# A decoder block on one core: gates evaluated one product late, attention outputs loaded earlier, w_out in two interleaved couples

## The chip, the core and the metric

The kernel runs on one core of a Trainium2 chip. A core has five engines with an instruction queue each, worked off in order: TensorE (PE, matrix products, with its weight loads PEld beside them), VectorE (DVE), ScalarE (ACT), GpSimd (POOL) and SyncE (SP), which here issues every DMA transfer. An engine that comes to an instruction whose inputs are not there waits, and all that is queued behind it on that engine waits too. Products are collected in PSUM, eight banks of 128x512 numbers; all else lies in SBUF. The metric is the time of one execution in microseconds (us), the median of three runs: 1360.38 us before (1358.13 to 1365.16).

## The reference

All is float32; sequence and model width are 1024, the FFN width is 2816. Cut to what matters here:

```
u    = rmsnorm(x, norm1_g)
proj = u @ w_in          # aq, ak, av, mqk, mv, mo, mi, mf, ga, gm
ya   = sliding_window_attention(aq, ak, av, sinks) @ w_attn_branch
h    = mlstm_chunkwise(silu(conv(mqk)), mv, mi, mf)      # 8 chunks of 128
h    = rmsnorm(h) * sigmoid(mo)
ym   = h @ w_mlstm_branch
x    = x + (sigmoid(ga) * ya + sigmoid(gm) * ym) @ w_out
f    = rmsnorm(x, norm2_g)
x    = x + (silu(f @ w_ffn_gate) * (f @ w_ffn_up)) @ w_ffn_down
out  = rmsnorm(x, final_norm_g)
```

## The kernel before

Activations lie transposed (channels on the partitions, 1024 tokens along the row, cut in two halves of 512). Every float32 operand is split into a rounded part and the rest (`split`: ACT writes the first, DVE or POOL the second, line 72/73), and each product is three matmuls: high by high, high by low, low by high (lines 776 to 778 and 108 to 110).

The program goes in stages. First the input projections with attention and the mLSTM recurrence (about 0 to 345 us in the trace); beside the recurrence, whose chunks are the loop over `c`, two of the four operand groups for the next stage are prepared (`u_load`, `operand`). Then the gates mo and gm (345 to 472), the two branch products (472 to 574; "o" is the attention output, "hh/hl" the split of the gated h), w_out with the residual (574 to 740), the FFN's gate and up products (740 to 1300) and the down projection.

Gates, w_out and FFN use a Strassen-Winograd scheme. A *pair* n is a 256-row block of weights against all 1024 tokens; its 2x2 block product needs seven products instead of eight, numbered 1 to 7, each of 12 matmuls of 128x512 (`seven`). A pair gives four quarters ij = 0 to 3, each 128 channels by 512 tokens. Pairs 0 to 5 are the gates (PG), 6 to 9 are w_out (PO), 10 to 31 the FFN (PF). `product7` runs one product and combines its sums: product 1 is copied to "v" (line 801), product 5 to "d" (806), "w" (809, then POOL in 810) is quarter 3, "c" (817) are quarters 1 and 2. Even pairs collect in banks "mm" and odd ones in "mb" (three each), product 5 in "st" (two). `prep` makes a product's weights four products ahead: sums "s_" on POOL (line 760), then a split into "whi"/"wlo" (five buffers each). `load_pair` reads a pair's weights from memory: "wraw" (two buffers) and "wr2" ("wr" in the trace; two blocks).

The order of products is the list SEQ: the first two pairs of a stage are interleaved (`first_two`), the others follow one by one in ORDER. Work is recorded in program order and each engine's queue follows it closely; so where the recording of a pair's loads, of a sigmoid or of a store stands sets where it comes in the queue.

Three consumers matter. In the gates, `out_gate` multiplies a quarter by Rt (line 824, on DVE for quarters 0 and 1, on POOL for the others), takes the sigmoid on ACT (825) and either multiplies h (829) or stores gm to memory (827). Line 849 (`load_o`) reads the attention output back after product 7 of the last gate pair, `split_o` splits it beside products 2 and 3, and the loop behind the gates' stage splits h. In w_out, `out_x` adds the residual "xr" (line 944, on DVE for quarter 0, on POOL for the others), writes the FFN's operand "f" (ACT, 947), and passes the previous quarter to `to_tokens`: four PE transposes into an "st" bank (922), copies by ACT and DVE (927, 929), four squares with sums on ACT (932) and a store. All operands that the FFN derives from f are made beside the products of pair 9 (`last_x`).

Of the kernel before, what the change touches and what calls it, by code (L numbers as in the profile page):

```python
# [17 lines left out]
D = 1024  # L18
# [14 lines left out]
def hybrid_block(ctx, tc, xT, xt, par, g3row, cst, abias, w_fm, w_mv, w_br, w_pr, w_dn, out):  # L33
# [621 lines left out]
    for a, b in ((PO, PF), (PF, PN)):  # L655
        SEQ += first_two(a, (1, 5), (6, 7), (2, 3, 4)) + [(n, i) for n in range(a + 2, b) for i in ORDER]
# [23 lines left out]
    def u_load(kt, late=False):  # L680
        for k in (2 * kt, 2 * kt + 1):
# [6 lines left out]
            else:  # L688
                U_[k] = blk("xz")
                nc.sync.dma_start(out=U_[k], in_=xT[k])  # L690
                A.activation(U_[k], U_[k], AF.Copy, scale=scale)

    ml_a(0)
    run(gai)
    for c in range(NT):
        if c + 1 < NT:
            ml_a(c + 1)
        ml_b(c)
        run(gai)
        if c > 0:  # L700
            ml_c(c - 1)
        if c in (2, 5):
            u_load(c // 3)
        if c in (3, 6):
            for i in (5, 6, 7, 4):
                operand("u", i, c // 3 - 1, U_)
# [31 lines left out]
    def load_pair(n):  # L738
# [4 lines left out]
        r.append([half("wr2", "hs", 3), half("wr2", "hs", 3)] if n == PG + 1 else blk("wr2"))  # L743
        for i in range(2):
            if n == PG + 1 and i:
# [6 lines left out]
    def prep(g):  # L752
        n, i = SEQ[g]
        if i == 6 and n + 1 not in (PG + 1, PO, PO + 1, PF, PF + 1):
            load_pair(n + 1)
# [64 lines left out]

    def out_gate(n, ij, c):
        j, h = 2 * n + ij // 2, ij % 2
        dst = c if ij else ev_("c")
        (V if ij in (0, 1) else G).tensor_tensor(dst, c, Rt[:, hs(h)], ALU.mult)
        A.activation(dst, dst, AF.Sigmoid)
        if j >= 4:
            nc.sync.dma_start(out=gmd[j - 4, :, hs(h)], in_=dst)
            return
# [32 lines left out]
    for g in range(NSG):  # L861
# [3 lines left out]
        if g in (0, 1, 3, 8):  # L865
            todo_u.pop(0)()
        product7(n, i, lambda n, ij: ev_("c"), out_gate)
        if n == PO - 1:
            if i == 7:
# [4 lines left out]
            elif i in (2, 3):  # L874
                split_o(i - 2, 0)
                split_o(i - 2, 1)
                if i == 2:
                    wt_y[0] = weights(w_br[0], 4)

# [39 lines left out]
    def to_tokens(xc, j, h):  # L919
        pt = st_ps()  # L920
        for t in range(4):
            T.transpose(pt[:, t * P:(t + 1) * P], xc[:, t * P:(t + 1) * P], idn)
        x_, junk = work("x2"), work("junk")
# [6 lines left out]
        for t in range(4):  # L930
            c = slice(t * P, (t + 1) * P)
            A.activation(junk[:, c], x_[:, c], AF.Square, accum_out=ss2[:, h * 4 + t, j:j + 1])
# [8 lines left out]
    def out_x(n, ij, c):  # L941
# [7 lines left out]
        if len(later) > 1:  # L949
# [71 lines left out]
    def dprep(c):  # L1021
# [11 lines left out]
        elif i == 4:  # L1033
# [6 lines left out]
    last_x = {1: [(1, 0), (1, 1)], 6: [(1, 2), (5, 0)], 5: [(5, 1), (5, 2)], 7: [(6, 0), (6, 1)],  # L1040
              2: [(1, 3), (6, 2), (7, 0)], 3: [(5, 3), (6, 3)], 4: [(7, 1), (7, 2), (7, 3)]}
    res_at = {1: 3, 6: 0, 5: 1, 7: 2}
    prep(NSG + 2)
    prep(NSG + 3)
    for g in range(NSG, len(SEQ)):
# [3 lines left out]
        if n < PF:  # L1049
            if i in res_at:  # L1050
# [194 lines left out]
```

## Time and profile before

| | before |
|---|---|
| median of 3 runs | 1360.38 us |
| the profiled execution | 1365.96 us, span 1364.2 us |
| PE busy | 1297.9 us, 95% of the span |
| DVE, ACT, POOL busy | 61%, 45%, 45% |
| granted TensorE clock, mean | 0.98 |

The span runs from the first to the last instruction of the profiled execution; what lies around it is 1.8 us. Times in rows are us from the span's start. PE is busy nearly always, so what can be won on the other engines shows only where PE has a gap, or where it works at the lower granted clock. A PE instruction's own duration includes its drain: in a run of 128x512 matmuls each starts about 0.23 us behind the last.

### The profile page before, as it was taken

Reading aid. Unit: us, or ns where it says so; the run is one execution under the profiler, and the core shown is the slowest. Engines: PE = TensorE matmul, PEld = TensorE weight load, DVE = VectorE, ACT = ScalarE, POOL = GpSimd, SP = SyncE. Lnnn points to the kernel's source line nnn. Section 1 sums busy time; section 2 is a strip of 40 time slices with the busy share of each in tenths; the row PEclk is TensorE's granted clock in tenths of the full one; section 3 lists DMA queues with packets and bytes.
Section 4 is the critical chain, followed back from the end, with each engine's and each line's share of the span. In section 5 each row is a group of like instructions: output and inputs, shape, how many; then the busy total and the mean of one; then the engine's idle time right before and its main releaser. Section 6 shows DMA issues by size and latency. Waiting matters only on the chain.

```text
span 1364.2 us, 17154 instructions
## 1 busy us (share of the span) xinstructions
PE 1297.9 (95%) x5970; PEld 1052.6 (77%) x5970; DVE 837.8 (61%) x1335; ACT 619.7 (45%) x1271; POOL 613.5 (45%) x480
## 2 busy tenths in 40 slices
PE   9999999999999979979779999999999999999986
PEld 7888998777777768857668888888888888888865
DVE  5369763566854464575795555556555565664795
ACT  5369864356523442247663333333233343555322
POOL 0245533231644333554556655566556535700470
PEclk9999999999999989989989999999999999999998
DMA  8111113302312453214413222332322249973761
GB/s 323 55 60 33 48 32 121 119 31 93 131 39 88 170 200 131 90 49 135 123 47 103 86 101 101 116 116 101 116 72 91 101 155 324 343 261 93 258 216 62
DMA packets 77799, 168.31 MB, mean 123 GB/s; under 512 B 8080, under 2 KB 16528, under 8 KB 77712
## 3 DMA queue, kind: packets, MB, share of 16 engines
q1 hardware_dynamic: 77712, 167.22, 35.8%
q8 instruction: 47, 0.77, 0.2%
q14 instruction: 40, 0.33, 0.1%
HBM read 128.13 MB, written 39.06 MB: 123 GB/s over the span
## 4 chain that ended last, share of the span: by engine, by line
PE 48%; DVE 6%; POOL 3%; ACT 3%; issue 2%; DMA 2%; SPq 0%; DVEq 0%; POOLq 0%; ACTq 0%
PE mm L777 6%; PE mm L778 6%; PE mm L776 5%; PE mb L777 5%; PE mb L776 5%; PE mb L778 5%; PE st L776 4%; PE st L777 4%; PE st L778 4%; DVE xzl L73 1%; DMA ld<-hd__5307 1%; PE mb L110 1%; PE mb L108 1%; PE mb L109 1%; DVE wlo L73 1%
## 5 line engine op out<-in xcount | busy, mean ns | idle before, releaser
L73 DVE TENSOR_TENSOR xzl<-ld,xzh 128x1024 fp32r<-128x1024 f32 x77 | 116.3, 1540 | 65.2 <-ACT xzh L72 53.3
L72 ACT ACTIVATE whi<-wraw 128x512 fp32r<-128x512 f32 (+1 forms) x124 | 77.2, 627 | 132.0 <-PE st L777 46.6
L73 DVE TENSOR_TENSOR wlo<-wraw,whi 128x512 fp32r<-128x512 f32 (+1 forms) x96 | 80.5, 841 | 42.4 <-ACT whi L72 42.3
L72 ACT ACTIVATE xzh<-ld 128x1024 fp32r<-128x1024 f32 x77 | 79.6, 1055 | 58.0 <-DMA ld<-in_w_dn_dram 18.6
L810 POOL TENSOR_TENSOR w<-w,d 128x512 f32<-128x512 f32 x32 | 50.3, 1572 | 119.4 <-DVE w L809 109.1
L108 PE MATMUL mm<-uh,whi 128*128 128x512 f32 x256 | 103.4, 407 | 0.5 <-ACT whi L72 0.5
L109 PE MATMUL mm<-ul,whi 128*128 128x512 f32 x256 | 102.2, 400 | 0.0
L110 PE MATMUL mm<-uh,wlo 128*128 128x512 f32 x256 | 101.9, 398 | 0.0
L776 PE MATMUL mb<-zf,whi 128*128 128x512 f32 x220 | 87.6, 398 | 0.0
L778 PE MATMUL mb<-zf,wlo 128*128 128x512 f32 x220 | 87.3, 397 | 0.1
L777 PE MATMUL mb<-zf,whi 128*128 128x512 f32 x220 | 87.3, 397 | 0.0
L776 PE MATMUL mm<-zf,whi 128*128 128x512 f32 x220 | 86.9, 395 | 0.0
L777 PE MATMUL mm<-zf,whi 128*128 128x512 f32 x220 | 86.8, 394 | 0.0
L778 PE MATMUL mm<-zf,wlo 128*128 128x512 f32 x220 | 86.7, 394 | 0.0
L776 PE MATMUL st<-zf,whi 128*128 128x512 f32 x176 | 70.2, 399 | 0.0
L777 PE MATMUL st<-zf,whi 128*128 128x512 f32 x176 | 70.1, 398 | 0.0
L778 PE MATMUL st<-zf,wlo 128*128 128x512 f32 x176 | 69.9, 397 | 0.0
L981 ACT ACTIVATE sg<-sg 128x512 f32<-128x512 f32 x44 | 27.7, 629 | 74.6 <-DVE sg L980 38.3
L108 PEld LDWEIGHTS mm<-uh,whi 128*128 128x128 f32 x256 | 49.1, 192 | 12.5 <-ACT whi L72 1.8
L110 PEld LDWEIGHTS mm<-uh,wlo 128*128 128x128 f32 x256 | 48.9, 191 | 11.6 <-DVE wlo L73 0.2
L777 PE MATMUL mm<-xzl,xzh 128*128 128x512 f32 x132 | 53.0, 402 | 4.9 <-DVE xzl L73 4.9
L109 PEld LDWEIGHTS mm<-ul,whi 128*128 128x128 f32 x256 | 49.0, 192 | 10.3
(766 smaller groups left out, 3805.0 us busy)
## 6 DMA issues: line engine op xcount, KB each, us to landing
ld<-hd__5307 SPq DMA_DIRECT2D x77, 256.0 KB, 4.6
lz<-in_w_dn_dram SPq DMA_DIRECT2D x66, 256.0 KB, 5.3
wraw<-in_w_pr_dram SPq DMA_DIRECT2D x32, 512.0 KB, 3.7
wr<-in_w_pr_dram SPq DMA_DIRECT2D x31, 512.0 KB, 5.5
hd__5307<-hs SPq DMA_DIRECT2D x44, 256.0 KB, 2.1
hd__5307<-sg SPq DMA_DIRECT2D x33, 256.0 KB, 2.3
ld<-in_w_dn_dram SPq DMA_DIRECT2D x33, 256.0 KB, 4.5
wraw<-in_w_fm_dram SPq DMA_DIRECT2D x16, 512.0 KB, 3.8
```

What stands on the lines that cost most here:

```text
L72: A.activation(hi, src, AF.Copy)
L73: eng.tensor_tensor(lo, src, hi.bitcast(F32), ALU.subtract)
L108: T.matmul(ps, ah, bh, start=(i == 0), stop=False)
L109: T.matmul(ps, ah, bl, start=False, stop=False)
L110: T.matmul(ps, al, bh, start=False, stop=(i == n - 1))
L776: T.matmul(ps, xh, zh, start=start, stop=False, skip_group_check=more)
L777: T.matmul(ps, xh, zl, start=False, stop=False, skip_group_check=more)
L778: T.matmul(ps, xl, zh, start=False, stop=stop, skip_group_check=more)
L810: G.tensor_tensor(e["w"], e["w"], e["d5"], ALU.subtract)
L981: A.activation(dst, dst, AF.Silu)
```

## The change

SEQ runs pairs 8 and 9 interleaved like 6 and 7. Their weights are loaded behind product 4 of pairs 6 and 7. In the gates the odd pairs 1, 3 and 5 put their second weight block into two half tiles ("hs") instead of a wr2 block, with one DMA each; the sigmoid of a quarter is recorded one product later than its multiply and a gm store one more (`late`). The attention output is loaded after product 1 of pair 5 instead of product 7 and split one block per product. `u_load` scales x on POOL instead of ACT, and its pieces are spread over chunks 2 to 6. In w_out, transposes go into "mm"/"mb" banks, a quarter waits two places instead of one in `later`, and the square is written back into the bank (no "junk" tile); the FFN operands are spread over the products of pairs 8 and 9 (`early_f`), and the residual is loaded by a list (`need`), three quarters ahead.

```diff
--- before.py
+++ after.py
@@ -652,8 +652,9 @@
 
     SEQ = first_two(PG, (1,), (2,), (5,), (6, 7), (3, 4)) + [(n, i) for n in range(PG + 2, PO) for i in ORDER]
     NSG = len(SEQ)
-    for a, b in ((PO, PF), (PF, PN)):
-        SEQ += first_two(a, (1, 5), (6, 7), (2, 3, 4)) + [(n, i) for n in range(a + 2, b) for i in ORDER]
+    for a in (PO, PO + 2, PF):
+        SEQ += first_two(a, (1, 5), (6, 7), (2, 3, 4))
+    SEQ += [(n, i) for n in range(PF + 2, PN) for i in ORDER]
     fz = {}
 
     def z_of(n):
@@ -688,22 +689,22 @@
             else:
                 U_[k] = blk("xz")
                 nc.sync.dma_start(out=U_[k], in_=xT[k])
-                A.activation(U_[k], U_[k], AF.Copy, scale=scale)
+                G.tensor_scalar(U_[k], U_[k], scale, 1.0, ALU.mult, ALU.mult)
 
     ml_a(0)
     run(gai)
+    pieces = [lambda kt=kt, i=i: operand("u", i, kt, U_) if i else u_load(kt) for kt in range(2) for i in (0, 5, 6, 7, 4)]
     for c in range(NT):
         if c + 1 < NT:
             ml_a(c + 1)
+        if 2 <= c < 7:
+            pieces.pop(0)()
         ml_b(c)
         run(gai)
         if c > 0:
             ml_c(c - 1)
-        if c in (2, 5):
-            u_load(c // 3)
-        if c in (3, 6):
-            for i in (5, 6, 7, 4):
-                operand("u", i, c // 3 - 1, U_)
+        if 2 <= c < 7:
+            pieces.pop(0)()
     ml_c(NT - 1)
     run(gai, 16)
     ph_a.close()
@@ -740,9 +741,10 @@
         if n in raws or n >= PN:
             return
         r = [wp.tile([P, 1024], F32, name="wraw", tag="wraw", bufs=2)]
-        r.append([half("wr2", "hs", 3), half("wr2", "hs", 3)] if n == PG + 1 else blk("wr2"))
+        odd = n < PO and n % 2
+        r.append([half("wr2", "hs", 3), half("wr2", "hs", 3)] if odd else blk("wr2"))
         for i in range(2):
-            if n == PG + 1 and i:
+            if odd and i:
                 for k in range(2):
                     nc.sync.dma_start(out=r[i][k], in_=w_pr[n, i, :, hs(k)])
             else:
@@ -751,7 +753,9 @@
 
     def prep(g):
         n, i = SEQ[g]
-        if i == 6 and n + 1 not in (PG + 1, PO, PO + 1, PF, PF + 1):
+        if (n, i) in ((PO, 4), (PO + 1, 4)):
+            load_pair(n + 2)
+        elif i == 6 and n + 1 not in (PG + 1, PF + 1) and not PO <= n + 1 <= PF:
             load_pair(n + 1)
         x11, x12, x21, x22 = raws[n]
 
@@ -818,13 +822,18 @@
             out(n, ij, c)
 
 
+    late = []
+
     def out_gate(n, ij, c):
         j, h = 2 * n + ij // 2, ij % 2
         dst = c if ij else ev_("c")
         (V if ij in (0, 1) else G).tensor_tensor(dst, c, Rt[:, hs(h)], ALU.mult)
+        late.append(lambda: sig_gate(dst, j, h))
+
+    def sig_gate(dst, j, h):
         A.activation(dst, dst, AF.Sigmoid)
         if j >= 4:
-            nc.sync.dma_start(out=gmd[j - 4, :, hs(h)], in_=dst)
+            late.append(lambda: nc.sync.dma_start(out=gmd[j - 4, :, hs(h)], in_=dst))
             return
...
@@ -864,18 +873,24 @@
             prep(g + LA)
         if g in (0, 1, 3, 8):
             todo_u.pop(0)()
+        now = late[:]
         product7(n, i, lambda n, ij: ev_("c"), out_gate)
+        for f_ in now:
+            late.remove(f_)
+            f_()
         if n == PO - 1:
-            if i == 7:
+            if i == 1:
                 for h in range(2):
                     for p in range(2):
                         load_o(h, p)
                 load_g(0)
-            elif i in (2, 3):
-                split_o(i - 2, 0)
-                split_o(i - 2, 1)
+            elif i in (5, 7, 2, 3):
+                k = (5, 7, 2, 3).index(i)
+                split_o(k // 2, k % 2)
                 if i == 2:
                     wt_y[0] = weights(w_br[0], 4)
+    while late:
+        late.pop(0)()
...
@@ -917,10 +932,10 @@
     F_, xres, later = {}, {}, []
 
     def to_tokens(xc, j, h):
-        pt = st_ps()
+        pt = bank(j // 2 % 2, 0)
         for t in range(4):
             T.transpose(pt[:, t * P:(t + 1) * P], xc[:, t * P:(t + 1) * P], idn)
-        x_, junk = work("x2"), work("junk")
+        x_ = work("x2")
         for q in range(2):
             c = slice(q * 256, (q + 1) * 256)
             if q == 0:
@@ -929,7 +944,7 @@
                 V.tensor_copy(x_[:, c], pt[:, c])
         for t in range(4):
             c = slice(t * P, (t + 1) * P)
-            A.activation(junk[:, c], x_[:, c], AF.Square, accum_out=ss2[:, h * 4 + t, j:j + 1])
+            A.activation(pt[:, c], pt[:, c], AF.Square, accum_out=ss2[:, h * 4 + t, j:j + 1])
         nc.sync.dma_start(out=x2d[h * 4:(h + 1) * 4, :, j * P:(j + 1) * P].rearrange("t p c -> p t c"),
                           in_=x_.rearrange("p (t c) -> p t c", t=4))
 
@@ -946,7 +961,7 @@
             F_[j] = blk("f")
         A.activation(F_[j][:, hs(h)], xc, AF.Copy, scale=prm[:, C_G2 + j:C_G2 + j + 1])
         later.append((xc, j, h))
-        if len(later) > 1:
+        if len(later) > 2:
             to_tokens(*later.pop(0))
 
 
@@ -1037,9 +1052,14 @@
         dop[c] = hi, lo
 
     todo = [("m", i, kt, mg) for i in (6, 7, 2, 3, 4) for kt in range(4)]
-    last_x = {1: [(1, 0), (1, 1)], 6: [(1, 2), (5, 0)], 5: [(5, 1), (5, 2)], 7: [(6, 0), (6, 1)],
-              2: [(1, 3), (6, 2), (7, 0)], 3: [(5, 3), (6, 3)], 4: [(7, 1), (7, 2), (7, 3)]}
-    res_at = {1: 3, 6: 0, 5: 1, 7: 2}
+
+    early_f = {(PO + 2, 5): [(1, 0)], (PO + 3, 1): [(1, 1)], (PO + 3, 5): [(5, 0)], (PO + 2, 6): [(5, 1)],
...
+    need = [(n + k, ij) for n in (PO, PO + 2) for k, ijs in ((0, (3,)), (1, (3,)), (0, (0, 1, 2)), (1, (0, 1, 2))) for ij in ijs]
+    for _ in range(3):
+        load_res(*need.pop(0))
...
@@ -1047,18 +1067,16 @@
         if g + LA < len(SEQ):
             prep(g + LA)
         if n < PF:
-            if i in res_at:
-                load_res(n, res_at[i])
-            if n == PF - 1 and i == 6:
-                load_pair(PF)
-            if n == PF - 1 and i == 2:
-                load_pair(PF + 1)
+            if (n, i) in ((PF - 1, 7), (PF - 1, 2)):
+                load_pair(PF + (i == 2))
             product7(n, i, lambda n, ij: ev_("c"), out_x)
-            if n == PF - 1:
-                for i_, kt in last_x[i]:
-                    operand("f", i_, kt, F_)
-                if i == 4:
-                    todo = [("f", i_, kt, F_) for i_ in (2, 3, 4) for kt in range(4)]
+            if i in (7, 2, 3, 4) and need:
+                load_res(*need.pop(0))
+            for i_, kt in early_f.get((n, i), ()):
+                operand("f", i_, kt, F_)
+            if (n, i) == (PF - 1, 4):
+                todo = [("f", 2, kt, F_) for kt in range(4)] + [("f", 3, kt, F_) for kt in (2, 3)]
+                todo += [("f", 4, kt, F_) for kt in range(4)]
         else:
             if i == 1 and n % 2 == 0:
                 sgs[n] = sgs[n + 1] = [x for _ in range(2) for x in halves(blk("sg"))]
@@ -1068,8 +1086,9 @@
             product7(n, i, dst_h, out_h)
             if later:
                 to_tokens(*later.pop(0))
-                V.tensor_reduce(rstd2, ss2, mybir.AxisListType.X, ALU.add)
-                rstd_of(rstd2, rstd2, D, NT)
+                if not later:
+                    V.tensor_reduce(rstd2, ss2, mybir.AxisListType.X, ALU.add)
+                    rstd_of(rstd2, rstd2, D, NT)
         if n == PN - 1 and i in (7, 2, 3):
             for c in {7: range(LP), 2: range(2), 3: range(2, LP)}[i]:
                 (dload if i == 7 else dprep)(c)
```

SP's queue in the gates, before (gmd are the gm stores, wr and wraw weights, o the attention output; wr_4112 and wr_4265 are the second blocks of pairs 4 and 5):

```order
L827 DMA gmd<-c 128x512
L749 DMA wr_4112<-in_w_pr_dram 128x1024
L827 DMA gmd<-w 128x512
L827 DMA gmd<-c 128x512 x2
L81 DMA wraw<-in_w_br_dram 128x512
L827 DMA gmd<-c 128x512
L749 DMA wr_4265<-in_w_pr_dram 128x1024
L827 DMA gmd<-w 128x512
L827 DMA gmd<-c 128x512 x2
L849 DMA o<-od 128x1024
L827 DMA gmd<-c 128x512
L849 DMA o<-od 128x1024 x3
```

and now:

```order
L751 DMA wraw<-in_w_pr_dram 128x1024
L749 DMA wr_4265<-in_w_pr_dram 128x512
L749 DMA wr_4266<-in_w_pr_dram 128x512
L751 DMA wraw<-in_w_pr_dram 128x1024
L751 DMA wr_4112<-in_w_pr_dram 128x1024
L836 DMA gmd<-w 128x512
L836 DMA gmd<-c 128x512 x2
L751 DMA wraw<-in_w_pr_dram 128x1024
L836 DMA gmd<-c 128x512
```

Both blocks now stand ahead of the first gm store, and pair 5's in two halves. ACT at the third of the gate pairs, before (whi is the split of a weight sum, L825 the sigmoid):

```order
L806 ACTIVATE d_4086<-st 128x512
L72 ACTIVATE whi<-s__4117 128x512
L825 ACTIVATE w<-w 128x512
L72 ACTIVATE whi<-s__4115 128x512
L825 ACTIVATE c<-c 128x512
L72 ACTIVATE whi<-s__4160 128x512
L825 ACTIVATE c<-c 128x512
```

and now:

```order
L810 ACTIVATE d_4088<-st 128x512
L72 ACTIVATE whi<-s__4117 128x512
L834 ACTIVATE w<-w 128x512
L72 ACTIVATE whi<-s__4115 128x512
L834 ACTIVATE c<-c 128x512
L72 ACTIVATE whi<-s__4159 128x512
L834 ACTIVATE c<-c 128x512
```

Line numbers apart (L834 is the sigmoid) the order of the kinds of work is the same here; s__4115 is pair 3's first sum in both. ACT at the end of the gates, before (oh and hh are the rounded parts of o and h, mg the branches' sigmoid):

```order
L72 ACTIVATE oh<-o 128x1024
L825 ACTIVATE w<-w 128x512
L72 ACTIVATE oh<-o 128x1024
L72 ACTIVATE whi<-wraw 128x512
L825 ACTIVATE c<-c 128x512
L72 ACTIVATE hh<-hT 128x2x256 x2
L72 ACTIVATE whi<-wraw 128x512
L72 ACTIVATE hh<-hT 128x2x256 x2
L825 ACTIVATE c<-c 128x512
L72 ACTIVATE hh<-hT 128x2x256 x3
L825 ACTIVATE c<-c 128x512
L72 ACTIVATE hh<-hT 128x2x256
```

and now:

```order
L72 ACTIVATE oh<-o 128x1024
L834 ACTIVATE w<-w 128x512
L72 ACTIVATE whi<-wraw 128x512
L834 ACTIVATE c<-c 128x512
L72 ACTIVATE hh<-hT 128x2x256 x4
L72 ACTIVATE whi<-wraw 128x512
L72 ACTIVATE hh<-hT 128x2x256
L834 ACTIVATE c<-c 128x512
L72 ACTIVATE hh<-hT 128x2x256
L72 ACTIVATE whi<-wraw 128x512
L834 ACTIVATE c<-c 128x512
L72 ACTIVATE hh<-hT 128x2x256 x2
```

The splits of o are done before the last sigmoids, and two of the eight splits of h stand behind the last one, where it was one.

POOL at the start of w_out, before (s__ are weight sums, L810 and L944 the two steps of a quarter w, wr_5383 and wr_5699 the second blocks of pairs 8 and 9):

```order
L760 TENSOR_TENSOR s__5578<-wraw,s__5386 128x512
L760 TENSOR_TENSOR s__5702<-wr_5383 128x512
L668 TENSOR_TENSOR mg<-mg 128x512
L760 TENSOR_TENSOR s__5704<-s__5702,wraw 128x512
L760 TENSOR_TENSOR s__5774<-wraw,wr_5383 128x512
L810 TENSOR_TENSOR w<-w,d_5372 128x512
L944 TENSOR_TENSOR w<-w,xr 128x512
L668 TENSOR_TENSOR mg<-mg 128x512
L810 TENSOR_TENSOR w<-w,d_5438 128x512
L944 TENSOR_TENSOR w<-w,xr 128x512
L760 TENSOR_TENSOR s__5831<-wraw,s__5704 128x512
```

and now (L764, L814 and L959 are the same steps; wr_5504 and wr_5608 belong to pairs 8 and 9):

```order
L764 TENSOR_TENSOR s__5562<-wraw,s__5388 128x512
L669 TENSOR_TENSOR mg<-mg 128x512
L814 TENSOR_TENSOR w<-w,d_5378 128x512
L959 TENSOR_TENSOR w<-w,xr 128x512
L669 TENSOR_TENSOR mg<-mg 128x512
L764 TENSOR_TENSOR s__5689<-wr_5504 128x512
L814 TENSOR_TENSOR w<-w,d_5436 128x512
L959 TENSOR_TENSOR w<-w,xr 128x512
L959 TENSOR_TENSOR c<-c,xr 128x512
L764 TENSOR_TENSOR s__5761<-wr_5608 128x512
L764 TENSOR_TENSOR s__5798<-s__5689,wraw 128x512
```

The first quarter of pair 6 no longer stands behind a weight sum of pair 8; the quarter of pair 7 stands behind one.

## Rows read from the trace of the kernel before

**Rows 1.** Windows: stretch, length, busy us (instructions) by engine, granted clock, DMA.

```profile
345.00:472.00 127.00, 122.65 (x517) 95.69 (x516) 74.53 (x102) 50.32 (x87) 61.30 (x44) 1.00 0.31 106
472.00:496.00 24.00, 14.90 (x51) 10.62 (x50) 13.57 (x21) 12.09 (x20) 4.73 (x2) 0.79 0.53 192
574.00:740.00 166.00, 141.08 (x587) 110.86 (x586) 117.97 (x149) 93.33 (x267) 89.37 (x60) 0.91 0.27 85
740.00:1300.00 560.00, 559.02 (x2413) 452.62 (x2411) 328.66 (x368) 213.83 (x330) 287.85 (x194) 1.00 0.44 153
```

**Rows 2.** Timeline of SP, end of the gates: start us, us, queue, line, transfer.

```profile
461.12 1.18 SPq L849 DMA_DIRECT2D o<-od  x1
```

**Rows 3.** Timeline, boundary to the branches; idle time and its releaser in brackets.

```profile
478.38 8.58 SPq L827 DMA_DIRECT2D gmd<-c  x3
...
481.75 0.68 DVE L817 TENSOR_TENSOR c<-mb,v 128x512 f32<-128x512 f32 x1
...
482.51 3.44 POOL L824 TENSOR_TENSOR c<-c,Rt 128x512 f32<-128x512 f32 x1 [10.77 <-DVE c L817]
485.99 0.63 ACT L825 ACTIVATE c<-c 128x512 f32<-128x512 f32 x1 [2.94 <-POOL c L824]
...
487.78 0.68 DVE L73 TENSOR_TENSOR wlo<-wraw,whi 128x512 fp32r<-128x512 f32 x1
...
488.52 0.79 PE L110 MATMUL mb<-hh,wlo 128*128 128x512 f32 x1 [6.73 <-DVE wlo L73]
```

**Rows 4.** Waits of POOL, 345 to 500 us: line, releaser, us in total, times, longest.

```profile
POOL s__4268 L760 <- DMA wr<-in_w_pr_dram: 7.9, 1, 7.9
...
POOL s__4417 L760 <- DMA wr<-in_w_pr_dram: 6.8, 1, 6.8
```

**Rows 5.** Timeline, one of the gaps in the gates.

```profile
413.78 0.63 ACT L825 ACTIVATE w<-w 128x512 f32<-128x512 f32 x1 [4.94 <-POOL w L824]
...
414.99 0.50 PE L776 MATMUL st<-zu,whi 128*128 128x512 f32 x1 [0.61 <-ACT whi L72]
```

**Rows 6.** Waits of PE, whole span: line, releaser, us in total, times, longest.

```profile
PE st L922 <- POOL c L944: 10.7, 4, 4.8
...
PE tp L590 <- ACT num L571: 6.1, 5, 1.7
...
PE st L922 <- POOL w L944: 4.6, 2, 3.9
...
PE st L776 <- ACT zm L72: 3.8, 1, 3.8
```

**Rows 7.** Timeline, first stall of w_out, and DVE a little later.

```profile
591.89 0.68 DVE L809 TENSOR_TENSOR w<-mm,v 128x512 f32<-128x512 f32 x1
...
594.47 1.28 POOL L760 TENSOR_TENSOR s__5704<-s__5702,wraw 128x512 f32<-128x512 f32 x1 [5.45 <-DMA wraw<-in_w_pr_dram]
...
599.61 0.72 ACT L947 ACTIVATE f<-w,prm 128x512 f32<-128x512 f32 x1 [8.42 <-POOL w L944]
...
600.90 0.50 PE L776 MATMUL mm<-zm,whi 128*128 128x512 f32 x1 [3.19 <-ACT zm L72]
...
607.87 1.74 DVE L73 TENSOR_TENSOR wlo<-wr,whi 128x512 fp32r<-128x512 f32 x1
```

**Rows 8.** The page, part 6: transfer, queue, count, KB each, median us to landing.

```profile
wr<-in_w_pr_dram SPq DMA_DIRECT2D x31, 512.0 KB, 5.5
```

**Rows 9.** Lines by form, ACT in w_out: count, busy us, mean ns, idle before.

```profile
L932 ACT ACTIVATE junk<-x 128x128 f32<-128x128 f32 x64 | 18.9, 299 | 5.8 <-DVE x L929 5.6
L72 ACT ACTIVATE zf<-f 128x512 fp32r<-128x512 f32 x28 | 16.3, 623 | 0.1
L932 ACT ACTIVATION_READ_ACCUMULATOR junk<-x 128x1 f32 x64 | 12.1, 189 | 0.0
```

**Rows 10.** Lines by form, POOL, whole span.

```profile
L810 POOL TENSOR_TENSOR w<-w,d 128x512 f32<-128x512 f32 x32 | 50.3, 1572 | 119.4 <-DVE w L809 109.1 <-issue 7.1 <-ACT x L927 3.2
...
L314 POOL TENSOR_SCALAR s<-s,den 128x256 f32<-128x256 f32 x56 | 27.2, 505 | 49.0 <-ACT vb L398 24.8 <-DVE den L312 9.9 <-ACT qs L288 7.8
```

More of the change, by code (lines that the diff above doesn't have):

```diff
@@ L1039, in hybrid_block @@
     todo = [("m", i, kt, mg) for i in (6, 7, 2, 3, 4) for kt in range(4)]
-    last_x = {1: [(1, 0), (1, 1)], 6: [(1, 2), (5, 0)], 5: [(5, 1), (5, 2)], 7: [(6, 0), (6, 1)],
-              2: [(1, 3), (6, 2), (7, 0)], 3: [(5, 3), (6, 3)], 4: [(7, 1), (7, 2), (7, 3)]}
-    res_at = {1: 3, 6: 0, 5: 1, 7: 2}
+    early_f = {(PO + 2, 5): [(1, 0)], (PO + 3, 1): [(1, 1)], (PO + 3, 5): [(5, 0)], (PO + 2, 6): [(5, 1)],
+               (PO + 2, 7): [(6, 0)], (PO + 3, 6): [(6, 1)], (PO + 3, 7): [(7, 0), (7, 1)], (PO + 2, 2): [(1, 2), (3, 0)],
+               (PO + 2, 3): [(3, 1), (5, 2)], (PO + 2, 4): [(6, 2)], (PO + 3, 2): [(1, 3), (7, 2)],
+               (PO + 3, 3): [(5, 3)], (PO + 3, 4): [(6, 3), (7, 3)]}
+    need = [(n + k, ij) for n in (PO, PO + 2) for k, ijs in ((0, (3,)), (1, (3,)), (0, (0, 1, 2)), (1, (0, 1, 2))) for ij in ijs]
+    for _ in range(3):
+        load_res(*need.pop(0))
     prep(NSG + 2)
```

## The prediction

> **What bounds the kernel now.** I read the stages first. The windows give a length, PE's busy time with its count of matmuls, and the granted clock for each stage [rows 1]. The FFN stage is the yardstick: 560 us for 2413 matmuls, 0.232 us each at clock 1.00, hence 2.785 us for a product of 12. PE bounds it and nothing is to be had there. Against this pace:
> - Gates: 517 x 0.232 = 120.0 of 127 us, so 7.0 lost, at full clock.
> - Boundary to the branches: 51 x 0.232 = 11.8 of 24 us, so 12.2 lost, at clock 0.79.
> - w_out: 587 matmuls, 64 of them transposes a quarter as wide. 523 x 0.232 + 64 x 0.058 = 125.1 of 166 us, so 40.9 lost, at clock 0.91.
>
> That is 60 us in three places, and the change works on all three. Next the waits of PE: transposes on POOL's sums 10.7 and 4.6 us, matmuls on ACT's "zm" 3.8 [rows 6] and 3.2 [rows 7]. These four belong to w_out and make 22.3 us. The other 18.6 us lost there go mostly to matmuls at the lower of the two clock levels (1.2 of 2.4 GHz) behind the gaps: a mean of 0.91 over 166 us is 0.09 x 166 = 15 us. So a microsecond of named wait there has cost 40.9 / 22.3 = 1.83 us all in; I price what remains with that factor.
>
> **Gates.** Three weight sums of POOL waited 6.8 to 7.9 us for a pair's second weight block (the longest and the shortest of them in [rows 4]), and POOL's later work came late with them: the sigmoid of "w" waited 4.94 us for POOL, and the weight split behind it opened a gap on PE [rows 5]. The order shows that ACT's rows at that place are as before, split still behind sigmoid; so recording the sigmoid late does nothing there, and the gain must come from SP, where both blocks now stand ahead of the first gm store. The halves cost SP one more issue a pair, while it has nothing else to do. A POOL that no longer waits 7 us has "w" ready 5 us before ACT asks. I take 5.5 of the 7.0, bounds 2 and 7.
>
> **Boundary.** The last gap ends with a chain: DVE takes the last quarter c at 481.75, behind splits of o and h; POOL multiplies it for 3.44 us; ACT's sigmoid follows at 485.99, behind it the last split of h, and behind that DVE's weight split at 487.78, for which PE waits 6.73 us [rows 3]. Smaller waits for splits of o stand in front of it. The o loads were issued at 461.12 and after [rows 2]. They are now recorded three products earlier, 8.4 us, so about 452.7, and one block is split per product while gates still run. The last gate product ends near 472.2, so c was taken 9.5 us late. Without o's splits in front I count from that end: c 0.7, its subtraction done at 1.4, POOL 3.44 at worst to 4.8, sigmoid 5.4, two splits of h on ACT 6.6, DVE 7.3. PE first does two products of o (5.6 us) and needs the last rows of h late in the fourth, at about 9.7. So 2.4 us to spare although two splits of h stand behind the last sigmoid where it was one. The gm stores after that sigmoid waited up to 8.58 us in SP's queue [rows 3], with the branches' gv loads behind them; the same walk puts them at 6, before the second branch's operands are needed. Saved: 11 of 12.2, bounds 6 and 12.
>
> **w_out.** In the first stall POOL waits 5.45 us for raw weights of pair 8, the quarter of pair 6 stands behind it, ACT's f waits 8.42 us for POOL, and the "zm" split stands behind f: PE idles 3.19 us [rows 7]. The new order takes pair 8's sums out from in front of pair 6's quarter, so this stall goes. But one sum of pair 8 (on wr_5504) now stands ahead of pair 7's quarter. On SP its load is behind a residual load that waits for POOL's first quarter. DVE has pair 6's w at 592.6, two POOL steps of 1.3 us end at 595.2 [rows 7], and with 5.5 us to landing [rows 8] the block is there at 600.7. Sum, w and residual make 3.9 us, f 0.7 and zm 0.6 more: 605.9. PE stood at the first stall at 597.7 and comes to this zm one product later, at 600.5. A stall of 5.4 us stays; 3.5 if it lands 2 us sooner.
>
> The transposes' waits come from running one quarter behind. With two in `later` each quarter has two products (5.6 us) more, and the longest wait was 4.8 [rows 6], so these 15.3 us should go. What is late next is ACT in the second couple: 64 squares at 299 ns with 189 ns to read each sum (31 us over the stage), and FFN splits at 623 ns [rows 9]. Six of the couple's eight quarters come out of its last six products; with f, squares, copies and a weight split (0.72 + 1.95 + 1.0) each, and ten FFN splits, I count 28 us of ACT work beside nine products (25 us) of PE. As a square is now written back into its bank, a product may have to wait for a bank until ACT is through: four squares hold it 4 x 0.488 = 2 us, and two or three such waits make 4.5 us.
>
> Remaining waits 5.4 + 4.5 = 9.9 us, times 1.83 is 18 us, so about 22 of 40.9 are saved. With 3.5 us of waits it would be 34; with 18 us (every second of the 16 transposed quarters holding PE 2 us beside a stall) 8. I take 22, the walk's value.
>
> **mLSTM stage.** PE waited 6.1 us there for ACT's "num" [rows 6]. Spreading the operands takes a few splits out of ACT's way; four scalings of 128x1024 go to POOL. Nothing in this trace has that shape: by the 505 ns of a 128x256 one it is at most 2.0 us each, by two 128x512 of two inputs 3.1 [rows 10], in a stage where POOL has room. I take 1 us gained, bounds 4 lost and 4 gained.
> By the Trainium skill, "SBUF — State Buffer", section "Who interferes with whom", a DVE instruction with two SBUF inputs contends with a GpSimd instruction that reads SBUF. The trace agrees: a DVE split took 0.68 us beside an idle POOL and 1.74 beside a busy one [rows 3, 7]. By the rule this move would slow DVE; it is the fourth rival below.
>
> The rest (FFN operands built earlier, residual loads by list, the sum of squares reduced once instead of twice) lies beside full products; if that cover fails it is inside the 18 us above. I cost it at nothing.
>
> **Sum.** 5.5 + 11 + 22 + 1 = 39.5 us. The profiled execution took 1365.96, so 1326.5 in its terms; it lay 5.6 us above the median 1360.38. Against the median: **1321 us**. All waits at their good ends (7 + 12 + 34 + 4 = 57) would give 1303, all at their bad ends (2 + 6 + 8 - 4 = 12) 1348.
>
> **Rivals.**
> 1. *The wait in w_out is only moved* to POOL's sum behind the weight load and to ACT's queue in the second couple. For it: the order row just named and ACT's load. Against it: transposes get 5.6 us. w_out saves 8: 25.5 in all, 1335 us.
> 2. *The branches still wait for h's splits*, since two of them stand behind the last sigmoid: POOL's c was 3.44 us, and 2.4 us of slack are few. The boundary saves 4 instead of 11: 1328 us.
> 3. *Slower: banks held by squares.* Each of 16 transposed quarters takes a bank that the products use and frees it when ACT has done the last square. If ACT is as late as in the longest wait on record, 4.8 us, times 1.83 that is 8.8 us a quarter. The other stages save 16.5, so w_out must lose over 40.9 + 16.5 + 6.8 = 64 us: it decides from 8 of the 16 on. Then 70.4 - 57.4 = 13 us slower, 1373 us. For it: ACT's load. Against it: three banks a side, and in the interleaved order two products of the other pair lie between. The Trainium skill ("ScalarE: Activation LUTs", "Step-by-step: what each stage is for") holds that ACT writes to PSUM with less latency than to SBUF, if TensorE doesn't need most of PSUM; no row here has a square into PSUM, and that condition is this rival.
> 4. *DVE pays for POOL's scalings.* At most 4 x 3.1 = 12.4 us of POOL work, beside which about seven DVE operations run 1.06 us longer: 7 us, of which DVE's own slack hides some. mLSTM then loses 4 to 6: 1327 us.
> 5. *It doesn't do what it says:* SP's in-order queue holds the early loads behind other waits, so that POOL and ACT come as late as before. Gates and boundary give 5, w_out nothing: 1355 us.
>
> **Chances.** Forecast 0.57 (own range 1309 to 1331), rival 1 0.22, 2 0.08, 3 0.04, 4 0.05, 5 0.04. The range 1307 to 1345 leaves out rivals 3 and 5 and the outer tails of the others. 0.5% (6.8 us) is what a measurement here can tell from no change. Faster by more: the forecast and rivals 1, 2, 4, less a tail: 0.91. Within: rival 5 and that tail: 0.05. Slower: 0.04.
>
> **What would show it.** Right: no DMA wait of POOL's weight sums in the gates; no gap over 1 us between the gates' last product and the branches' fourth; in w_out no wait of a transpose for POOL over 1 us, one wait of about 5 us for zm in the first couple, and the stage some 144 us long. Wrong: gaps of PE whose releaser is a square in w_out (rival 3, or 1 if few), a wait for hh or hl behind the last sigmoid (2), more waits for num in the mLSTM stage, with DVE splits at 1.7 us beside POOL's scalings (4), unchanged windows in the gates (5).

## The result and the profile after

The changed kernel takes 1340.16 us (median of 4 runs, 1338.44 to 1341.87) against 1362.77 for the kernel before on the same chip (4 runs, 1358.13 to 1365.48): a ratio of 0.9838, 95% interval 0.9802 to 0.9873. That is 22.6 us, by the ratio 1.6%, faster, where 39.5 us were forecast. The profiled executions differ by 27.0 us (spans 1364.2 and 1337.2).

The windows of the kernel after, in the columns of [rows 1], stage by stage; w_out now lies from 560 to 714:

```profile
345.00:472.00 127.00, 124.17 (x535) 99.60 (x534) 89.07 (x112) 59.57 (x102) 65.52 (x44) 1.00 0.36 121
472.00:490.00 18.00, 18.00 (x79) 14.55 (x78) 13.44 (x21) 9.65 (x15) 5.58 (x4) 1.00 0.78 289
560.00:714.00 154.00, 137.03 (x588) 109.44 (x587) 117.49 (x151) 92.17 (x267) 91.93 (x60) 0.92 0.31 94
714.00:1274.00 560.00, 559.08 (x2413) 452.57 (x2411) 326.22 (x368) 213.98 (x330) 286.37 (x194) 1.00 0.45 153
```

At the boundary PE is busy without a gap at full clock, where [rows 1] had 51 matmuls in 24 us. The FFN's pace is the same to the last matmul. w_out, counted as in the prediction (524 x 0.232 + 64 x 0.058 = 125.3 of 154 us), still loses 28.7 us of the 40.9, at clock 0.92. The waits of PE there (line, releaser, us in total, times, longest; line numbers in the kernel after lie 4 to 15 further on; L937 are the transposes, L146 brings the row scale of the FFN):

```profile
PE st L780 <- ACT zm L72: 6.0, 1, 6.0
PE mb L780 <- ACT mb L947: 4.4, 1, 4.4
PE mb L937 <- issue: 2.8, 1, 2.8
PE mm L146 <- POOL rstd L141: 2.7, 1, 2.7
PE st L781 <- DVE zf L73: 0.5, 1, 0.5
PE mb L937 <- POOL c L959: 0.4, 1, 0.4
```

The transposes' waits for POOL ([rows 6], 15.3 us) are down to 0.4. What stands in their place is one wait for zm of 6.0 us, where two of 3.8 and 3.2 stood before, and two new ones, for banks: L947 is the square, now in the bank "mb".

To place a change of time I cut each run's trace at four points: two matmuls of the mLSTM recurrence (from its first step to the last chunk but one), PE's first matmul on o (start of the branches), its first on zm (w_out) and its first on the third pair of the FFN. Lengths in us of one execution each, and the median with its ratio to the kernel before on that chip (the ratio is taken over all runs of both and differs a little from the quotient of the two medians):

| kernel | mLSTM | branches | w_out | median | ratio, 95% interval |
|---|---|---|---|---|---|
| before | 77.6 | 101.7 | 165.9 | 1362.77 | 1 |
| after | 81.1 | 89.1 | 153.5 | 1340.16 | 0.9838 (0.9802 to 0.9873) |
| e1 o loaded late | 82.2 | 89.1 | 153.2 | 1340.48 | 0.9864 (0.9837 to 0.9890) |
| e2 whole blocks | 80.2 | 94.3 | 155.0 | 1346.69 | 0.9904 (0.9883 to 0.9925) |
| e3 sigmoids at once | 81.4 | 89.1 | 153.5 | 1340.29 | 0.9857 (0.9835 to 0.9879) |
| e4 mLSTM as before | 77.5 | 89.1 | 153.8 | 1336.68 | 0.9824 (0.9800 to 0.9849) |
| e5 before + half tiles | 78.7 | 88.9 | 164.6 | 1347.89 | 0.9891 (0.9866 to 0.9915) |
| e6 = e1 and e2 | 82.8 | 100.3 | 154.4 | 1353.45 | 0.9931 (0.9907 to 0.9955) |
| e7 squares in SBUF | 81.1 | 89.1 | 154.7 | 1341.55 | 0.9842 (0.9816 to 0.9868) |
| e8 f late | 82.5 | 89.1 | 149.9 | 1334.07 | 0.9789 (0.9765 to 0.9813) |
| e9 scalings on ACT | 78.8 | 89.1 | 153.0 | 1335.65 | 0.9847 (0.9833 to 0.9862) |
| e10 = e4 and e8 | 79.2 | 89.1 | 149.6 | 1331.82 | 0.9817 (0.9802 to 0.9831) |
| e11 = e10, three places | 76.0 | 89.1 | 154.6 | 1337.06 | 0.9863 (0.9845 to 0.9881) |
| e12 one place | 82.8 | 89.1 | 158.0 | 1345.32 | 0.9873 (0.9829 to 0.9918) |

The kernel before took 1360.55 beside e1 to e4, 1363.91 beside e5 to e8, 1356.79 beside e9 to e11 and 1362.76 beside e12, 7 us apart, so medians of different groups do not compare closely and the ratios are to be used; within a group medians do. Of the stages, w_out lies at 153.0 to 155.0 us in the runs that leave it as changed (after, e1 to e4, e6, e9), so a difference of 1 or 2 us there says nothing. By these cuts the 27.0 us of the profiled pair are: branches 12.6, w_out 12.4, gates 4.3 (from the first z product to the branches 112.5 and 108.2 us), the FFN and after 0.9, and up to the gates 3.2 lost.

### The profile page after: what moved, and what is told of

Its sections match the earlier page's. It is cut to its first block, busy times and chain, and to the rows that moved or that the text cites. A ratio compares the mean times of both kernels' runs of the same rounds, so it can differ in the third digit from the quotient of the medians.

```text
span 1337.2 us, 17162 instructions
## 1 busy us (share of the span) xinstructions
PE 1287.6 (96%) x5970; PEld 1050.5 (79%) x5970; DVE 846.2 (63%) x1335; ACT 615.3 (46%) x1267; POOL 619.1 (46%) x484
## 4 chain that ended last, share of the span: by engine, by line
PE 53%; DVE 8%; POOL 4%; ACT 3%; issue 3%; DMA 2%; SPq 0%; DVEq 0%; POOLq 0%; ACTq 0%
PE mm L781 6%; PE mm L782 6%; PE mm L780 6%; PE mb L781 6%; PE mb L780 6%; PE mb L782 6%; PE st L780 4%; PE st L782 4%; PE st L781 4%; DVE xzl L73 1%; DVE wlo L73 1%; PE mb L110 1%; PE mb L109 1%; PE mb L108 1%; PE mm L108 1%
## 5 line engine op out<-in xcount | busy, mean ns | idle before, releaser
L814 POOL TENSOR_TENSOR w<-w,d 128x512 f32<-128x512 f32 x32 | 52.9, 1655 | 136.0 <-DVE w L813 116.6
L73 DVE TENSOR_TENSOR wlo<-wraw,whi 128x512 fp32r<-128x512 f32 (+1 forms) x96 | 83.3, 871 | 43.4 <-ACT whi L72 43.0
L110 PE MATMUL mm<-uh,wlo 128*128 128x512 f32 x256 | 101.7, 397 | 0.0
L314 POOL TENSOR_SCALAR s<-s,den 128x256 f32<-128x256 f32 (+1 forms) x64 | 32.8, 532 | 52.7 <-ACT vb L398 25.3
```

Source lines behind the costliest of these rows:

```text
L73: eng.tensor_tensor(lo, src, hi.bitcast(F32), ALU.subtract)
L110: T.matmul(ps, al, bh, start=False, stop=(i == n - 1))
L314: G.tensor_scalar(sv[:, hh, c0:256], sv[:, hh, c0:256], den[:, hh:hh + 1], 1.0, ALU.mult, ALU.mult)
L814: G.tensor_tensor(e["w"], e["w"], e["d5"], ALU.subtract)
```

## The experiments

**e1: the attention output loaded late again.**

```diff
-            if i == 1:
+            if i == 7:
                 (four load_o, load_g)
-            elif i in (5, 7, 2, 3):
-                k = (5, 7, 2, 3).index(i)
-                split_o(k // 2, k % 2)
+            elif i in (2, 3):
+                split_o(i - 2, 0)
+                split_o(i - 2, 1)
```

> The changed kernel with one part undone: the attention output is loaded after product 7 of pair 5 and split two blocks at a time beside products 2 and 3, as before; the sigmoids stay one product late. Theory: the early load of o is what closed the boundary, so the stretch between the last gate product and the branches loses its 12 us again: about 1352 us, with gaps on PE in front of the splits of o and one of several us for a weight split behind h. Rival: the late sigmoids and the earlier end of POOL's work in the gates did it; then at most 3 us come back, about 1343 us.

Nothing came back: branches 89.1 as in the kernel after. The theory was wrong. (The gates are 2.4 us longer, 110.6 at a granted clock of 0.98; e11 and e12, whose gates are those of the kernel after, have 109.9 at 0.98 too, so that is not put down to the edit.)

**e2: pairs 3 and 5 in whole blocks again.**

```diff
-        odd = n < PO and n % 2
+        odd = n == PG + 1
```

> The changed kernel with one part undone: pairs 3 and 5 put their second weight block in a whole block again. Theory: the gates' gaps came from POOL's weight sums waiting for that block (6.8 to 7.9 us each), so POOL waits for a DMA return, the gates' stage loses about 4 us again: 1344 us, with POOL waits of about 7 us. Rival: the late sigmoids keep ACT's weight splits on time even with POOL late; then no gap returns: 1340 us.

The waits of POOL came back, in the columns of [rows 4]:

```profile
POOL s__4113 L764 <- DMA wr<-in_w_pr_dram: 7.5, 1, 7.5
POOL s__4266 L764 <- DMA wr<-in_w_pr_dram: 7.4, 1, 7.4
POOL s__4415 L764 <- DMA wr<-in_w_pr_dram: 7.0, 1, 7.0
```

With them came 3.1 us in the gates, near the 4 expected, and 5.2 in the branches, which neither the theory nor the rival had. The gates' length alone would not show much, for it lies anywhere from 108.2 to 110.6 us in the runs with half tiles. PE's waits do: three for weight splits come back, which the kernel before and e6 have too and no run with half tiles has:

```profile
PE st L780 <- ACT whi L72: 2.5, 3, 1.0
```

**e3: sigmoids and stores at once.**

```diff
-        late.append(lambda: sig_gate(dst, j, h))
+        sig_gate(dst, j, h)
...
-            late.append(lambda: nc.sync.dma_start(out=gmd[...], in_=dst))
+            nc.sync.dma_start(out=gmd[...], in_=dst)
```

> The changed kernel with one part undone: sigmoid and store of a gate quarter are recorded at once, not one and two products late. Theory: the order on ACT is hardly another, so this is worth nothing: 1340 us within 2, no new gap in the gates. Rival: the lateness is what keeps weight splits from standing behind sigmoids that wait; then 3 to 5 us of gaps return in the gates and some at the branches: 1344 us.

1340.29 against 1340.16 (ratios 0.9857 and 0.9838, their intervals overlap), stages alike: worth nothing that shows, as the unchanged rows of ACT's order said.

**e5: the kernel before with half tiles alone.**

```diff
+        odd = n < PO and n % 2
-        r.append([half(...), half(...)] if n == PG + 1 else blk("wr2"))
+        r.append([half(...), half(...)] if odd else blk("wr2"))
...
-            if n == PG + 1 and i:
+            if odd and i:
```

> The kernel before with one line of the change: the second weight block of the gate pairs 3 and 5 goes into two half tiles. New theory, from e1 (nothing came back) and e2 (7 us came back, 5 of them at the branches): a pair that no longer holds a whole block lets both its own weights and the o loads be issued early, whatever line records them. Then this alone gives the gates' 4 us and all or most of the boundary's 12: 1346 us, o loads issued 15 us or more before the branches. Rival: it takes the earlier recording of the o loads as well, each part having covered for the other; then the boundary keeps 5 us or more of gaps: 1352 us.

16.0 us faster than the kernel before by this one edit (1347.89 against 1363.91; 12 to 18 by the interval), branches 88.9, gates 108.8: the theory holds in its time. Put into the kernel before, the half tiles of two pairs alone give 16.0 us, where the whole change gives 22.6. The first load of o on SP's queue shows how. In e1 (half tiles, recorded late), the kernel after (half tiles, recorded early) and e2 (whole blocks, recorded early); the columns are those of [rows 2]:

```profile
440.79 0.32 SPq L858 DMA_DIRECT2D o<-od  x1
```

```profile
439.25 0.32 SPq L858 DMA_DIRECT2D o<-od  x1
```

```profile
460.29 1.14 SPq L858 DMA_DIRECT2D o<-od  x1
```

With the 461.12 of [rows 2] (blocks, late) these make a table of two by two: the line that records the load moves it by 1 to 2 us, the half tiles by about 20. That is the first of four loads; the other three start at 463.08 to 464.08 before and at 452.25 to 453.17 in the kernel after.

What stands in front of the load tells the two apart. Before, and in e5:

```profile
444.41 0.33 SPq L749 DMA_DIRECT2D wr<-in_w_pr_dram  x1
457.00 0.32 SPq L827 DMA_DIRECT2D gmd<-w  x1
458.04 2.98 SPq L827 DMA_DIRECT2D gmd<-c  x2
```

```profile
438.39 0.32 SPq L850 DMA_DIRECT2D o<-od  x1
447.07 0.32 SPq L828 DMA_DIRECT2D gmd<-w  x1
448.11 2.99 SPq L828 DMA_DIRECT2D gmd<-c  x2
451.38 0.32 SPq L850 DMA_DIRECT2D o<-od  x1
```

In the kernel before the load stands behind three gate stores, the first of which holds SP for 12.2 us until ACT's sigmoid is done, and is issued as soon as the last of them is. In e5 it stands ahead of these stores, at the place where the second block of pair 5 stood (444.41), and like that block's load it follows a weight split of DVE that has just been done reading a block (at 438.36, and at 444.38 before). So the queue does not follow the recording here: e5 records the load behind a product of pair 5 that ends near 462. The blocks of o and the weight blocks come from one pool ("blk"); with pairs 3 and 5 out of it, o takes the block that pair 5's weights had. That the pool sets the load's place on the queue is read from the program; these rows agree with it, but no run changes the pool and nothing else.

**e6: both undone, e1 and e2.**

> The changed kernel with both undone: o loaded after product 7 of pair 5, and whole blocks for pairs 3 and 5. Theory: without the half tiles the line of the load matters, so the boundary is as in the kernel before, 12 us lost, and the gates lose 3: 1354 us. Rival: something else of the change (sigmoids late, the residual loads by list) holds part of it; then it stays near e2's 1347.

As expected, 1353.45, branches 100.3. With whole blocks the order does matter (94.3 with one split of o per product, 100.3 with two); with half tiles it is hidden. The change had two covers for one wait, and either part undone by itself shows too little: none and 5.2 of the 11.2 us that both bring back.

**e4 and e9: the mLSTM stage.** e4 takes all of it back, e9 only the scalings:

```diff
-                G.tensor_scalar(U_[k], U_[k], scale, 1.0, ALU.mult, ALU.mult)
+                A.activation(U_[k], U_[k], AF.Copy, scale=scale)
```

> The changed kernel with the mLSTM stage as before: x scaled on ACT, operand pieces bunched in chunks 2, 3, 5 and 6. Theory: the spread pieces put operand sums in front of the recurrence's own small steps on POOL and splits in front of them on DVE, which cost 2.9 us up to the start of the gates: 1337 us, PE's waits for num in this stage 6 us instead of 8.6. Rival: POOL's scalings slow DVE beside them; the same time, but then DVE's steps beside the scalings are long in the changed kernel (a next run keeps the spread and moves only the scalings). Second rival: the 2.9 us are chance, and it stays at 1340.

> The changed kernel with only the scalings of x in the mLSTM stage put back on ACT; the operand pieces stay spread over chunks 2 to 6. Theory: it is the spread (operand sums of POOL and splits of DVE in front of the recurrence's small steps) that costs the 3 us up to the gates, not the scalings: they took 1.1 us each on POOL; so 1340 us and the same start of the gates' z products, near 363. Rival: the scalings beside DVE are the cost; then those products start near 360 as in e4, 1337 us.

The ratio of e4 lies within the interval of the kernel after, though its four runs (up to 1337.65) are all shorter than those of e1 and e3 on the same chip (from 1338.83). The stage tells more: all eight runs with POOL's scalings have 80.2 to 82.8 us, all six with ACT's (before, e4, e5, e9, e10, e11) 76.0 to 79.2. e9 keeps the spread and has 78.8, so it is the scalings that cost: my theory of the spread fell, the rival stands. Where it happens, POOL's row and DVE's in the kernel after (start us, us, engine, line, work):

```profile
273.90 1.14 POOL L692 TENSOR_SCALAR xz<-xz,prm 128x1024 f32<-128x1024 f32 x1
```

```profile
274.14 3.47 DVE L606 TENSOR_SCALAR num<-num,mden 128x128 f32<-128x128 f32 x4
```

And the same four steps of DVE in e9, with POOL idle:

```profile
273.54 0.88 DVE L606 TENSOR_SCALAR num<-num,mden 128x128 f32<-128x128 f32 x4
```

Four small steps of the recurrence take 2.6 us more while POOL scales and sums beside them. In the next chunk POOL's sums, which follow its scalings, stand in front of its own small step (L141), and DVE waits for that 2.36 us, in e9 1.12:

```profile
288.24 1.24 DVE L604 TENSOR_TENSOR mden<-mden,mss 128x4 f32<-128x4 f32 x1 [2.36 <-POOL mss L141]
```

So a little of the first theory, sums in front of the recurrence's steps, is in it too. PE's waits for ACT's num are 8.6 us in all, against 6.1 in [rows 6] and 5.8 in e9.

**e7: squares from SBUF.**

```diff
-        x_ = work("x2")
+        x_, junk = work("x2"), work("junk")
...
-            A.activation(pt[:, c], pt[:, c], AF.Square, accum_out=...)
+            A.activation(junk[:, c], x_[:, c], AF.Square, accum_out=...)
```

> The changed kernel with the squares of w_out taken from the token tile in SBUF and written to a work tile, so that a transpose's bank is free after the two copies; its banks are mm and mb as changed. Theory: banks held by squares cost the changed kernel two gaps on PE (2.8 and 4.4 us) in the second couple and the lower clock behind them, so 8 to 12 us go: 1330 us, no wait of PE for a square. Rival: ACT's queue is the bound there and the same products wait for another of its instructions, or the two work tiles a quarter now takes hold the copies up; 1338 to 1342 us, with PE waiting for copies or weight splits at the same places.

No wait of PE for a square is left, and w_out takes 154.7: the rival's time, but not the waits that it named. PE now waits for POOL's quarters and longer for the row scale of the FFN:

```profile
PE mm L146 <- POOL rstd L141: 5.9, 1, 5.9
PE st L780 <- ACT zm L72: 5.1, 1, 5.1
PE mb L937 <- POOL c L959: 3.7, 1, 3.7
PE mm L937 <- POOL c L959: 1.8, 2, 1.4
...
```

The bank waits were real, but without them PE waits elsewhere for the same engines: 20.7 us in all, against 16.8. Whether the second work tile that the edit brings back has a part in it, no run separates.

**e8: f of quarters 3 one product later.**

```diff
-        A.activation(F_[j][:, hs(h)], xc, AF.Copy, scale=...)
+        f_ = lambda: A.activation(F_[j][:, hs(h)], xc, AF.Copy, scale=...)
+        late.append(f_) if ij == 3 else f_()
...
+            now = late[:]
             product7(n, i, lambda n, ij: ev_("c"), out_x)
+            for f_ in now:
+                late.remove(f_)
+                f_()
```

> The changed kernel with ACT's FFN operand f of each quarter 3 recorded one product later. Theory: the 6.0 us gap in the first couple comes from ACT standing at f until POOL has the quarter, with the zm splits and through them DVE's next quarter behind it; then the gap goes, with some 3 us of lower clock behind it: 1332 us. Rival: POOL's quarter is late by itself (a weight sum and its load stand in front of it), so f late moves the wait to the products that need zm anyway: 1339 us.

It is 1334.07, w_out 149.9 instead of 153.5. The wait for zm fell from 6.0 to 1.7 us in two, as the theory had it; of the 9 us expected there (6 and 3 of clock) the stage kept 3.6, the rest being given back to transposes and FFN splits:

```profile
PE mb L937 <- POOL w L959: 3.3, 2, 2.1
PE st L781 <- DVE zf L73: 2.3, 1, 2.3
PE mb L780 <- ACT mb L947: 2.3, 1, 2.3
...
PE mm L780 <- ACT zm L72: 1.1, 1, 1.1
...
PE st L780 <- ACT zm L72: 0.6, 1, 0.6
```

Of the 6.7 us by which its span is shorter than that of the kernel after, another 2.3 lie in the FFN and behind it, which the edit does not touch; e10, with the same edit, does not have them.

**e12: one place in front of the transposes, as before.**

```diff
-        if len(later) > 2:
+        if len(later) > 1:
```

> The changed kernel with a quarter waiting one place, as before, in front of its transposes; couples, early loads and FFN operands as changed. It tells what earned the 12 us that w_out won. Theory: the second place, for the transposes waited 15 us for POOL's residual sums before; then these waits come back and the stage is 160 us or longer: 1347 us or more. Rival: the interleaved couple, which puts a product of the other pair behind each quarter, so that the transposes come late enough with one place too; then the stage stays at 153 to 155 us: 1341 us.

Between the two: w_out 158.0. The transposes wait for POOL 15.6 us again, as much as before:

```profile
PE mb L937 <- POOL w L959: 8.2, 2, 5.5
...
PE mb L937 <- POOL c L959: 3.6, 1, 3.6
PE mm L937 <- POOL c L959: 2.9, 3, 2.0
...
PE mm L937 <- POOL w L959: 0.9, 1, 0.9
```

and yet only 4.5 us of the stage return. The waits for banks and the one of 6.0 us for ACT's zm are gone then; three for DVE's zm make 2.1, and the row scale is waited for 4.3. So taking away the second place costs 4.5 of the 12.4 us, and 7.9 come without it: from the couple, the FFN operands built earlier or the residual loads by list, which no run takes apart.

**e10 and e11: towards a better version.** e10 is e4 and e8 together; e11 has `len(later) > 3` on top.

> Both gains together: the mLSTM stage as before (e4) and f of quarters 3 one product later (e8), the rest as changed. Theory: they lie in different stages and add up: 1340 - 3.5 - 6 = 1330.5 us. Rival: one of the two was chance, or the earlier stage moves the transfers of the later one; 1334 us or more.

> As e10, and a quarter waits three places instead of two before its transposes. Theory: with f out of the way the transposes of w_out wait for POOL's residual sums (5 us in e8, with clock lost behind them); one product more takes most of these waits away: 1324 us. Rival: the quarters' tiles are held longer (seven of them for all), so products wait for a tile to be evicted into, or the later sum of squares holds the row scale at the start of the FFN up: 1330 us or more, with other waits of the same size.

e10 has both stages as its parts had them, 79.2 and 149.6 us, and a span of 1330.6 us against 1337.2. With e8 (1330.5) it is the shortest profile; its median is 25.0 us under the kernel before on its chip, but its ratio (0.9817) is not told from that of the kernel after, so that the two gains add up in the time is not shown. e8's 0.9789 lies below it, 29.8 us under the kernel before, with intervals that still overlap a little. e11 is 5.2 us slower than e10 beside it: the wait for the row scale went from 0.9 to 4.3 us, those for ACT's zm and for banks from 5.2 to 9.9. The rival was right.

## Why the prediction was right, and where it was off

The direction and the range held, but 1340 lies nearer rival 1's 1335 than the forecast's 1321, and outside the forecast's own 1309 to 1331. Of the 39.5 us, 27.0 came in the profiled pair: three steps fell short, one went over. By its steps:

**Gates, 5.5 forecast, 4.3 measured: right,** with its cause. POOL's waits for the second blocks are what opened the gaps (e2), the lateness of the sigmoids and stores does nothing that shows (e3): it is the tiles that bring the loads forward (e5). A wait of 4.3 us for pair 2's block, which the change leaves as it is, stays.

**Boundary, 11 forecast, 12.6 measured: right in size by luck, wrong in its cause.** The step "they are now recorded three products earlier, 8.4 us" failed: e1 records the loads late and they are issued from 440.79 on all the same. Three of the four do start near the forecast's 452.7 in the kernel after (452.25 on), but by another road. The half tiles, which I had counted for the gates alone, bring the first load of o forward by 20 us and the others by 9 to 12 (e5). The order listing showed o's place on SP's queue among the stores, but not that the tiles decide it; nor does it hold for these loads that the place of their recording sets their place in the queue, as the section on the kernel before has it.

**w_out, 22 forecast, 12.4 measured: the mis-sized term.** The factor of 1.83 was taken over the four longest waits. Over all of PE's idle time in the stage (length less busy time, [rows 1] and the windows above) it is 40.9 over 24.9 us, 1.64, before and 28.7 over 17.0, 1.69, after: it held. What was too small is the sum of the waits left: 9.9 forecast, 16.8 measured.
- "A stall of 5.4 us stays" in the first couple: it is 6.0, but the step to it failed. The block that I gave 5.5 us to land came 3.8 us after its issue and cost POOL 0.47 us. The chain in the kernel after is another:

```profile
581.33 0.72 ACT L962 ACTIVATE f<-w,prm 128x512 f32<-128x512 f32 x1 [3.86 <-POOL w L959]
581.96 2.18 ACT L72 ACTIVATE zm<-mg 128x512 fp32r<-128x512 f32 x4
```

```profile
582.61 3.60 DVE L73 TENSOR_TENSOR zm<-mg,zm 128x512 fp32r<-128x512 f32 x4 [2.06 <-ACT zm L72]
586.13 1.80 DVE L73 TENSOR_TENSOR wlo<-wraw,whi 128x512 fp32r<-128x512 f32 x1
587.84 0.68 DVE L813 TENSOR_TENSOR w<-mb,v 128x512 f32<-128x512 f32 x1
```

```profile
593.24 0.80 PE L780 MATMUL st<-zm,whi 128*128 128x512 f32 x1 [6.03 <-ACT zm L72]
```

  ACT stood at pair 6's f until POOL had the quarter, four zm splits queued behind it; DVE took their low parts late, and pair 7's own quarter only behind them, at 587.84, though its product had ended near 582.4. The weight split between took 1.80 us beside POOL's sum, where one took 0.68 beside an idle POOL [rows 3]. From there POOL, f and zm follow as I had them. e8 moves f out of the way and the wait falls to 1.7.
- "Two or three such waits make 4.5 us" for banks: 4.4 + 2.8 = 7.2 us (the "issue" wait ends within 0.1 us of the last square of its bank). The place was right. The 2 us for which four squares hold a bank were too few, since f and FFN splits, with what ACT waits for at them, stand between them in ACT's queue: 4.8 us in one case (638.18 to 642.98) and 4.1 in the other:

```profile
667.49 0.26 ACT L947 ACTIVATE mb<-mb 128x128 f32<-128x128 f32 x1
...
671.45 0.18 ACT L947 ACTIVATION_READ_ACCUMULATOR mb<-mb 128x1 f32 x1
```

  But e7 shows that the price is not the bank's: with free banks other waits of the same engines take the time.
- The wait at the row scale's products (L146), 2.7 us, was missing from my list; before, PE waited 2.3 us at the same place, for DVE.

**mLSTM, 1 gained forecast, 3.2 lost measured: the sign was wrong,** within the bounds given (4 lost). Rival 4 was the mechanism and was priced at 4 to 6. A scaling took 1.14 us, well under the bounds of 2.0 and 3.1, but DVE's small steps beside POOL took four times as long. It was these steps and not the splits that its sign had named: no split of DVE took over 0.69 us in this stage of the kernel after. By the Trainium skill ("SBUF — State Buffer", "Who interferes with whom") a tensor_scalar of DVE can contend with GpSimd too, when its operands allow a two-port mode, and not only an operation with two SBUF inputs. The four steps at 3.47 instead of 0.88 us agree with it, and I had weighed only the other half of the section.

Rival 2 (branches wait for h) and rival 3 (slower by banks) did not come: no gap at the branches, and two waits for banks (7.2 us), not eight quarters of 8.8 us. Rival 1 came by half: the wait at ACT's queue in the second couple is there, that for POOL's sum behind a load is not (0.47 us). The 12.4 us saved in w_out lie between its 8 and the forecast's 22; that the total came out near its 1335 owes as much to the 3.2 us lost in the mLSTM stage.

## What to carry to other kernels

Where a load is early or late, ask which tile it can have before you ask where it is recorded: two weight blocks moved into other tiles brought another consumer's loads forward by 9 to 20 us and, with what the gates gained themselves, earned 16.0 us in the kernel before. When two parts of a change cover the same wait, undoing each alone shows too little (0 and 5.2 us of 11.2 here); undo both, or add one to the old kernel. In a stage in which three in-order engines feed each other, a wait that is removed uncovers the next one. The second place takes 15 us of waits from the transposes, and the stage gets back 4.5 of them (e12); so price what remains, and expect more of it than you can name (9.9 us named, 16.8 measured).

## What the runs showed of the hardware

GpSimd scaled a 128x1024 tile in 1.14 us (four times in the kernel after), less than the 1.57 us of its sums of two 128x512 tiles in [rows 10]. Four 128x128 tensor_scalar steps of DVE took 0.88 us while POOL was idle and 3.47 beside its scalings and sums. A square read from and written to PSUM took 263 ns, from SBUF to SBUF 299 [rows 9]; the read of its sum took 188 and 189 ns, and the stage took 153.5 and 154.7 us (e7), which is within what it varies by.
